# A delta-rule recurrence in units of eight heads by 128 tokens, with its projections kept in DRAM

## The chip, the cores and the metric

One core of one Trainium2 chip. The metric is the device time of one execution in microseconds. The kernel before took 3592.41 us in the median of three runs (3590.86 to 3600.78).

## The reference

Three transformer-like blocks follow each other on one sequence of 1024 tokens by 1024 channels, all in float32. The change lies in the second block. That block normalises its input, projects it (`h @ w_in`, 2816 columns), and splits the result: 1792 columns feed a recurrence of eight heads of 64 channels, 1024 columns feed a gated convolution of 31 taps. Both results, 512 channels each, go through one output projection and are added to the input; then comes a feed-forward part.

```python
def rwkv7_recurrence(r, decay, k, v, a_vec, b_vec):
    def step(S, inp):
        r_t, w_t, k_t, v_t, a_t, b_t = inp
        sa = jnp.einsum('bhvk,bhk->bhv', S, a_t)
        S = S * w_t[:, :, None, :] + sa[..., :, None] * b_t[:, :, None, :] + v_t[..., :, None] * k_t[:, :, None, :]
        y = jnp.einsum('bhvk,bhk->bhv', S, r_t)
        return S, y
...
def second_block(x, ...):
        h = rmsnorm(x, norm_mix_g[l])
        p = h @ w_in[l]
        p_rwkv = p[..., :D_RWKV_IN]
        p_rwkv = p_rwkv + (token_shift(p_rwkv) - p_rwkv) * shift_mu[l]
        p_conv = p[..., D_RWKV_IN:]
        y_rwkv = rwkv7_group(p_rwkv, ...)
        y_conv = conformer_conv_group(p_conv, ...)
        x = x + jnp.concatenate([y_rwkv, y_conv], axis=-1) @ w_out[l]
        h = rmsnorm(x, norm_mlp_g[l])
        x = x + jnp.square(jax.nn.relu(h @ w_ff1[l])) @ w_ff2[l]
```

`rwkv7_group` makes r, k and v (512 columns each), the decay and the gates from the projection, runs the recurrence, normalises each head's output, adds a bonus term and multiplies by a gate.

## The kernel before

Activations lie channel-major: 128 channels on the partitions, tokens along the free dimension, in two halves of 512 tokens. A projection of 128 columns over one half is eight steps over the input channels, three matmuls each (operands are split into a high and a low part, `split`, lines 127 to 129), 24 matmuls of 128x512. `shift_mix` (line 1146 on) runs one such projection in eight parts and mixes it with its neighbour token: ScalarE scales it (L1160), VectorE adds the shifted copy (L1161). The weights come by `w_a`: one load of 512 KB on the SyncE queue (L139, two buffers `raw`), then the split on ScalarE (L128) and GpSimd (L129).

The recurrence is computed in chunks of 64 tokens, and its work in *units*. Before, a unit is one of two groups of four heads (two tiles of 128 channels) by 256 tokens, that is four chunks; a half has four units, group 0 twice, then group 1 twice. There are eight units. Each has

- a *preparation*, `rwkv_pre` (line 1200 on): decay, gates and norms, then the score matrices inside a chunk (`sa`, `sb`, L1285 and L1289), transposes, and `chunk_inverse` (L1437 to L1472), which inverts the eight 64x64 triangles with products of 32x32 blocks; its last matmuls are L1328. It yields some 31 times, and nearly every step needs the one before;
- a *chain*, `rwkv_chain` (line 1333 on): for each of the four chunks, state times `ar` (L1345), add (L1348), times the inverse (L1351), copy to `uv` (L1353, L1354), state update (L1359, L1363, with a product on GpSimd, L1356) and the output into `yp` (L1368, L1369). The state `z` goes from chunk to chunk and from unit to unit of a group;
- an *end*, `rwkv_post`: statistics on ScalarE and GpSimd (L1375 to L1390), transposes (L1401), gate, and a store into the DRAM tensor `mixd`.

In `mixers_2` (line 1559 on) three kinds of work are woven together. `drive` takes one step of each of its streams in turn, by the estimated numbers of steps `STEPS`: the chain and end of unit u, and the preparation of unit u+1. Beside them it feeds parts from a list, `work`, through `feed`; `SLOTS` says how many projections' worth of eight parts each drive gets (nine drives: preparation 0, then the eight chains). It also takes convolution taps from the list `taps`, `TAPS` in a drive: each convolution projection leaves 31 of them, two thirds on VectorE (L1511), one third on ScalarE and GpSimd (L1505, L1506). The steps of the streams have priority over the fed parts when the compiler orders the engines' queues.

The list `work` before: the two low-rank projections `L[0]`, the six projections `P[0]` of group 0, the convolution's `C[0]` to `C[3]` with `P[1]` between them, a reload of the second half's input, `L[1]`; then `P[2]` with the layer norm of the convolution's first half beside it (`("beside", N[0])`: one step of `conv_norm` for every six parts, `SIDE`; at `("join",)` the rest of the norm is run with no part beside it); then `C[4]` to `C[7]` with `P[3]`; then the output projection of the first half, `O[:4]`, with the second norm `N[1]` beside it; then a join, `mixed1` (the convolution's memory is given up, the second half's residual and mixed values are loaded) and `O[4:]`. `conv_norm` first takes the taps that are left, four a step, then transposes, normalises and stores eight blocks of 128 channels by 256 tokens with one buffer `cu` (L1548 to L1554, store L1571).

Eight projections' worth of parts run before the first drive. The output projection of the second half leaves out two of its eight channel tiles, those of the last unit; `ffn_2` adds them after the recurrence (L1775 to L1781). The projections r, k and v of a group stay in SBUF (`rkv`, six buffers of 128x2x512).

## Time and profile before

| what | value |
|---|---|
| median of three runs | 3592.41 us |
| the profiled execution, its own time | 3586.6 us |
| its span, first to last instruction | 3584.8 us |
| mean granted TensorE clock | 0.965 |
| TensorE busy | 96% |
| second block's recurrence with its projections | 1456 to 2237 us of the span |

The page's second part gives busy shares in 40 slices of 89.6 us each; slices 17 to 25 hold the stage of the change. A view by stretches gives, for each stretch of time, its length, each engine's busy time and count, the granted TensorE clock (1.00 is full speed, 0.50 half), the share of time that the DMA engines were busy, and GB/s. A view by groups gives for each line the busy time, the mean duration in ns of one instruction, and the idle time of its engine before it with what ended it. The timeline gives start and length of single instructions.

### The profile page before, as it was taken

The page shows a single profiled execution, that of the slowest core. Times are in us where ns is not written, and L with a number is a line of the kernel's source. Part 1 is how long each engine was busy: PE and PEld are TensorE (multiplying, and loading weights), DVE is VectorE, ACT ScalarE, POOL GpSimd, SP SyncE. Part 2 cuts the span into 40 slices and gives each one's busy share as a digit, 9 for nine tenths or more (in the row PEclk, how much of TensorE's full clock was granted, in tenths as well). Part 3 has the DMA queues.
Part 4 walks back from the last instruction along what each step waited for, and adds up shares of the span by engine and source line. Part 5 has one row for each costly group of instructions (what it writes and reads, how often), then busy time and mean ns, then how long its engine had stood idle before and what let it go on. Part 6 is the DMA issues. An engine that isn't in the chain of part 4 may idle for free.

```text
span 3584.8 us, 53990 instructions
## 1 busy us (share of the span) xinstructions
PE 3431.0 (96%) x22218; PEld 2742.5 (77%) x22218; DVE 2137.7 (60%) x3062; ACT 1152.0 (32%) x2191; POOL 1514.8 (42%) x1270
## 2 busy tenths in 40 slices
PE   8999889989999999999999998999999999998998
PEld 5877778777888887777776777888888887776877
DVE  7556785877577577675455643544444334577583
ACT  2322212232222222544444534312211134444561
POOL 3455552674344444554434634433333334344120
PEclk9999999999999999999979998999999999999999
DMA  5210035011111112412111223222222121110132
GB/s 190 71 52 24 27 124 212 30 42 48 47 47 48 47 47 71 156 43 83 44 40 45 65 74 121 92 75 72 71 68 65 50 77 51 42 33 30 51 106 77
DMA packets 256387, 247.26 MB, mean 69 GB/s; under 512 B 9490, under 2 KB 201598, under 8 KB 256138
## 3 DMA queue, kind: packets, MB, share of 16 engines
q1 hardware_dynamic: 256140, 243.80, 21.1%
q8 instruction: 175, 2.87, 0.3%
q14 instruction: 72, 0.59, 0.1%
HBM read 217.27 MB, written 26.49 MB: 68 GB/s over the span
## 4 chain that ended last, share of the span: by engine, by line
PE 69%; DVE 8%; POOL 3%; issue 3%; ACT 2%; DMA 1%; POOLq 0%; DVEq 0%; SPq 0%; ACTq 0%
PE mps L174 11%; PE mps L176 10%; PE mps L175 10%; PE dps L174 5%; PE dps L176 5%; PE dps L175 5%; PE mps L1148 3%; PE mps L1150 2%; PE mps L1149 2%; DVE cacc L927 2%; POOL hl L129 1%; PE ps L1285 1%; PE ps L1444 1%; PE yp L1988 1%; PE mps L1621 1%
## 5 line engine op out<-in xcount | busy, mean ns | idle before, releaser
L129 POOL TENSOR_TENSOR hl<-raw,hl 128x1024 fp32r<-128x1024 f32 x247 | 619.2, 2509 | 828.5 <-ACT hl L128 625.6
L174 PE MATMUL mps<-xt,hl 128*128 128x512 f32 x1888 | 755.0, 401 | 13.0 <-DVE cacc L940 8.1
L175 PE MATMUL mps<-xt,hl 128*128 128x512 f32 x1888 | 745.0, 395 | 0.0
L176 PE MATMUL mps<-xt,hl 128*128 128x512 f32 x1888 | 744.9, 395 | 0.0
L128 ACT CAST hl<-raw 128x1024 fp32r<-128x1024 f32 (+1 forms) x260 | 270.5, 1042 | 629.6 <-PE dps L176 443.9
L174 PEld LDWEIGHTS mps<-xt,hl 128*128 128x128 f32 x1888 | 358.7, 190 | 94.5 <-DVE cacc L940 8.6
L176 PEld LDWEIGHTS mps<-xt,hl 128*128 128x128 f32 x1888 | 357.7, 189 | 79.2 <-issue 0.9
L175 PEld LDWEIGHTS mps<-xt,hl 128*128 128x128 f32 x1888 | 358.8, 190 | 74.8 <-issue 1.0
L927 DVE SCALAR_TENSOR_TENSOR cacc<-apad,cols,cacc 128x1024 f32<-128x1024 f32 x176 | 345.5, 1967 | 112.3 <-ACT cacc L921 108.6
L174 PE MATMUL dps<-hl,hid 128*128 128x512 f32 x832 | 326.5, 393 | 1.5 <-DVE x L956 1.3
L176 PE MATMUL dps<-hl,hid 128*128 128x512 f32 x832 | 326.0, 392 | 0.6 <-POOL hid L849 0.6
L175 PE MATMUL dps<-hl,hid 128*128 128x512 f32 x832 | 326.2, 392 | 0.0
L1810 DVE TENSOR_TENSOR x<-x,dps 128x512 f32<-128x512 f32 x224 | 152.9, 687 | 175.2 <-PE dps L176 175.2
L174 PEld LDWEIGHTS dps<-hl,hid 128*128 128x128 f32 x832 | 156.1, 188 | 37.1 <-DVE x L956 1.7
L176 PEld LDWEIGHTS dps<-hl,hid 128*128 128x128 f32 x832 | 156.2, 188 | 35.7 <-POOL hid L849 1.1
L175 PEld LDWEIGHTS dps<-hl,hid 128*128 128x128 f32 x832 | 156.2, 188 | 34.3
L1797 DVE TENSOR_TENSOR ftmp<-ftmp 128x512 f32<-128x512 f32 x64 | 60.5, 947 | 177.2 <-ACT ftmp L1796 177.2
L1148 PE MATMUL mps<-xt,hl 128*128 128x512 f32 x352 | 162.3, 461 | 0.0
L174 PE MATMUL mps<-hl,xt 128*128 128x512 f32 (+1 forms) x368 | 140.1, 384 | 5.4 <-ACT xt L240 1.7
L1150 PE MATMUL mps<-xt,hl 128*128 128x512 f32 x352 | 144.5, 411 | 0.0
L1149 PE MATMUL mps<-xt,hl 128*128 128x512 f32 x352 | 144.3, 410 | 0.0
L175 PE MATMUL mps<-hl,xt 128*128 128x512 f32 (+1 forms) x368 | 139.3, 380 | 1.3 <-DVE hl L129 1.3
(518 smaller groups left out, 6480.0 us busy)
## 6 DMA issues: line engine op xcount, KB each, us to landing
raw<-in_w_in_dram SPq DMA_DIRECT2D x108, 512.0 KB
raw<-in_w_ff_dram SPq DMA_DIRECT2D x64, 512.0 KB
raw<-in_ffn_up_dram SPq DMA_DIRECT2D x44, 512.0 KB
adar<-in_ada_w_dram SPq DMA_DIRECT2D x32, 512.0 KB
raw<-in_w_out_dram SPq DMA_DIRECT2D x30, 512.0 KB
adar<-in_w_ada_dram SPq DMA_DIRECT2D x48, 256.0 KB
raw<-in_ffn_down_dram SPq DMA_DIRECT2D x22, 512.0 KB
xd<-x SPq DMA_DIRECT2D x16, 512.0 KB
```

Of the source, the lines that this page charges most:

```text
L128: nc.scalar.copy(hl[:, 0], raw)
L129: (low or nc.gpsimd).tensor_tensor(out=hl[:, 1], in0=raw, in1=f32(hl[:, 0]), op=ALU.subtract)
L174: self.nc.tensor.matmul(ps, lhsT=sh, rhs=mh, start=(i == 0), stop=False)
L175: self.nc.tensor.matmul(ps, lhsT=sh, rhs=ml, start=False, stop=False)
L176: self.nc.tensor.matmul(ps, lhsT=sl, rhs=mh, start=False, stop=(i == n - 1))
L927: nc.vector.scalar_tensor_tensor(out=acc, in0=pad[:, i // 3:i // 3 + 16, i % 3:i % 3 + 64], scalar=cw[:, i * 22 + j:i * 22 + j + 1], in1=a ...
L1148: nc.tensor.matmul(ps, lhsT=sh, rhs=xt[k][:, 0], start=(k == 0), stop=False)
L1149: nc.tensor.matmul(ps, lhsT=sh, rhs=xt[k][:, 1], start=False, stop=False)
L1150: nc.tensor.matmul(ps, lhsT=sl, rhs=xt[k][:, 0], start=False, stop=(k == 7))
L1285: nc.tensor.matmul(ps[:, c], lhsT=bk4[hp, b, c, h:h + 2].rearrange("p x s -> p (x s)"), rhs=ar4[hp, b, c].rearrange("p x s -> p (x s)"), s ...
L1797: nc.vector.tensor_tensor(out=v, in0=v, in1=v, op=ALU.mult)
L1810: nc.vector.tensor_tensor(out=xs[t][:, c], in0=xs[t][:, c], in1=ps, op=ALU.add)
```

## The change

A unit becomes all eight heads (four tiles of 128 channels) by 128 tokens, that is two chunks. The chain has two chunks a unit with eight heads side by side, one state tile instead of two, and its state update is an addition and a product on VectorE, with nothing on GpSimd. The r, k and v projections are stored in a DRAM tensor `rkvd` as they are made, all twelve of a half before the half's first unit, and a unit loads its 128 tokens of them back. The list of work, `SLOTS`, `TAPS` and `STEPS` change with it, and the second half's output projection now leaves out the last 128 tokens' recurrence channels instead of two channel tiles.

```diff
-SLOTS = (5, 5, 5, 6, 6, 6, 6, 5.5, 6.5)
+SLOTS = (5, 5, 5, 4, 4, 4, 3.5, 3, 8.5)
-STEPS = (20, 30)
-TAPS = 31
+STEPS = (12, 30)
+TAPS = 24
...
+        self.rkvd = dr.tile([1536, 1024], F32, name="rkvd")
...
-            res[0] = pool.tile([128, 512], F32, tag="tw", name="tw", bufs=1)
+            res[0] = pool.tile([128, 512], F32, tag="tw", name="tw", bufs=2)
...
+    def rwkv_proj(self, i, hf, xts, pool, psum, done):
+        out = []
+        def new():
+            out.append(pool.tile([128, 512], F32, tag="rkv", name="rkv", bufs=3))
+            return out[0]
+        yield from self.shift_mix(i, hf, xts, psum, new)
+        self.nc.sync.dma_start(out=self.rkvd[i * 128:(i + 1) * 128, hf * 512:hf * 512 + 512], in_=out[0])
+        done.append(i)
+
+    def rwkv_load(self, u, pool):
+        res = []
+        for n, i in (("k", 4), ("r", 0), ("v", 8)):
+            t = pool.tile([128, 4, 128], F32, tag="in" + n, name="in" + n, bufs=2)
+            self.nc.sync.dma_start(out=t, in_=self.rkvd[i * 128:(i + 4) * 128, u * 128:u * 128 + 128].rearrange("(b p) t -> p b t", p=128))
+            res.append(t)
+        return res
...
-        for b in range(2):
+        for b in range(4):
             nc.scalar.activation(out=sq[:, b], in_=k[:, b], func=ACT.Square, scale=col("k_k", b))
...
-        for b in range(2):
-            nc.vector.tensor_tensor_scan(out=sg[:, b], data0=m2["reset"].rearrange("p c t -> p (c t)"), data1=sg[:, b], initial=0.0,
-                                         op0=ALU.mult, op1=ALU.add)
+        nc.vector.tensor_tensor_scan(out=flat(sg), data0=m2["reset"].rearrange("p c t -> p (c t)"), data1=flat(sg), initial=0.0,
+                                     op0=ALU.mult, op1=ALU.add)
...
+        pairs = [(b, h, hp) for b in range(4) for h, hp in enumerate(hps)]
+        yp = psum.tile([128, 2, 4, 64], F32, tag="y", name="yp")
+        for c in range(2):
+            pc = psum.tile([128, 2, 4, 64], F32, tag="ch", name="pc")
+            for b, h, hp in pairs:
+                nc.tensor.matmul(pc[hp, 0, b], lhsT=ar[hp, 2 * b + c, 0], rhs=z[hp, b], start=True, stop=True)
             yield
+            rh = pool.tile([128, 4, 64], F32, tag="rh", name="rh", bufs=2)
+            nc.vector.tensor_tensor(out=rh, in0=pc[:, 0], in1=of(w1, c), op=ALU.add)
...
-            zg = pool.tile([128, 2, 64], F32, tag="zg", name="zg", bufs=1)
-            nc.gpsimd.tensor_tensor(out=zg, in0=z, in1=glv[:, :, c:c + 1].to_broadcast([128, 2, 64]), op=ALU.mult)
...
+            zn = pool.tile([128, 4, 64], F32, tag="z", name="z", bufs=3)
+            nc.vector.tensor_tensor(out=zn, in0=pc[:, 0], in1=z, op=ALU.add)
+            nc.vector.tensor_tensor(out=zn, in0=zn, in1=of(gl[:, :, None], c).to_broadcast([128, 4, 64]), op=ALU.mult)
...
-        P = [self.rwkv_proj(j % 2, j // 2, xts, lo, psum, projs[j]) for j in range(4)]
+        P = [[self.rwkv_proj(i, hf, xts, lo, psum, done) for b in range(4) for i in (4 + b, b, 8 + b)] for hf in range(2)]
-        work = L[0] + P[0]
+        work = L[0] + P[0][:4]
...
         def pre(u):
+            states[u] = yield from self.rwkv_pre(u % 4, loaded.pop(u), loras[u // 4][0], lw, r, psum)
+            if u < 7:
+                loaded[u + 1] = self.rwkv_load(u + 1, r)
...
-        work += C[0] + P[1][:3] + C[1] + P[1][3:] + C[2] + C[3] + [reload()] + L[1]
-        work += [("beside", N[0])] + P[2] + [("join",)] + C[4] + P[3][:3] + C[5] + P[3][3:] + C[6] + C[7] + [mixed()]
-        work += [("beside", N[1])] + O[:4] + [("join",), mixed1()] + O[4:]
-        more(4 * NPART)
+        work += C[0] + P[0][4:8] + C[1] + P[0][8:] + C[2] + C[3] + [reload()] + L[1]
+        work += [("beside", N[0])] + P[1] + [("join",)] + C[4] + C[5] + C[6] + C[7]
+        work += [mixed(), ("beside", N[1])] + O[:4] + [("join",), mixed1()] + O[4:]
+        for i in range(14 * NPART):
+            more(1)
+            if i % 2 and taps:
+                taps.pop(0)()
+        loaded[0] = self.rwkv_load(0, r)
...
-            for k in (4, 5, 6, 7, 0, 1):
+            for k in (4, 5, 6, 7):
                 self.load_mixed(mts1[k], k, 512, 512)
+            for k in range(4):
+                self.load_mixed(mts1[k], k, 512, 384)
...
-                terms = self.terms_b(xt, t, [hls[0][0]], 4, 256) + self.terms_b(xt, t, [hls[1][0]], hls[1][1], 256, 4)
+                terms = self.terms_b(xt, t, hls[:1], 4, 256, 4)
+                if hf == 0 or t < 3:
+                    terms += self.terms_b(xt, t, hls[1:], 4, 256)
...
-            hls = [self.w_b(a["w_out_2"][0], 256, 2, ch * 512, 512) for ch in range(2)]
...
+            for c0 in range(0, 1024, 256):
+                c = slice(c0, c0 + 256)
+                ps = psum.tile([128, 512], F32, tag="mm", name="mps")[:, :256]
+                self.mm3(ps, self.terms_b(mts, 3, [self.w_b(a["w_out_2"][0], 0, 4, c0, 256)], 4, 256))
+                nc.vector.tensor_tensor(out=xs[7][:, c], in0=xs[7][:, c], in1=ps, op=ALU.add)
```

In the preparation the loops over two tiles of 256 tokens become loops over four tiles of 128 (ScalarE's squares, tanh and scalings, VectorE's products by `k_k` and `r_k`, the low-rank matmuls), and the scan over the decay becomes one instruction instead of two. `chunk_inverse` only indexes its input in another way. The order of the work is now: eighteen projections' worth of parts before the first drive (`L[0]`, all of the first half's twelve, `C[0]`, `C[1]`), with one tap after every second part; then `C[2]`, `C[3]`, the reload, `L[1]`, all twelve of the second half beside the first layer norm, `C[4]` to `C[7]`, and the output projection as before.

## The prediction

> **What bounds the kernel now.** I read the page's totals first, then busy time by stretches, then single lines inside them.

> ```profile
> span 3584.8 us, 53990 instructions
> ...
> PE 3431.0 (96%) x22218; PEld 2742.5 (77%) x22218; DVE 2137.7 (60%) x3062; ACT 1152.0 (32%) x2191; POOL 1514.8 (42%) x1270
> ...
> PEclk9999999999999999999979998999999999999999
> ```

> TensorE (PE) is the bound by count, at full clock except in slices 20 to 24. Those slices hold the stage that the change rewrites, from 1456 to 2237 us. The next view cuts it: the projections ahead of the recurrence (first row), a piece of it with nothing else in it, the preparation of unit 0, the seven stretches in which chain u runs beside preparation u+1, the last chain, one hole, and a piece of the output projection. A stretch ends where the last matmul group of a preparation, line 1328, starts. Columns: length, busy us (count) of PE, PEld, DVE, ACT, POOL, then granted clock and DMA.

> ```profile
> 1456.00:1504.00 48.00, 48.00 (x232) 40.20 (x231) 19.73 (x32) 24.98 (x37) 27.57 (x27) 1.00 0.67 225
> 1480.00:1494.00 14.00, 14.00 (x63) 11.61 (x62) 4.08 (x9) 6.31 (x10) 5.71 (x7) 1.00 0.77 271
> 1504.00:1556.00 52.00, 46.43 (x742) 33.94 (x742) 39.79 (x68) 24.51 (x41) 31.39 (x24) 0.97 0.19 55
> 1556.00:1635.00 79.00, 78.07 (x1008) 55.97 (x1006) 42.57 (x86) 35.07 (x89) 37.08 (x32) 0.94 0.13 39
> 1635.00:1710.00 75.00, 73.94 (x1022) 53.07 (x1017) 48.87 (x94) 39.38 (x96) 43.88 (x39) 0.98 0.30 93
> 1710.00:1799.00 89.00, 86.61 (x1019) 62.59 (x1019) 40.05 (x87) 33.73 (x87) 33.95 (x32) 0.90 0.15 43
> 1799.00:1901.00 102.00, 100.83 (x1040) 75.19 (x1034) 53.05 (x110) 40.80 (x99) 39.86 (x36) 0.75 0.15 45
> 1901.00:1990.00 89.00, 85.90 (x1028) 61.28 (x1028) 45.36 (x88) 36.98 (x92) 39.18 (x32) 0.90 0.14 40
> 1990.00:2075.00 85.00, 78.88 (x1093) 61.10 (x1095) 63.10 (x110) 46.68 (x107) 58.63 (x45) 0.94 0.23 76
> 2075.00:2157.00 82.00, 77.94 (x1170) 65.47 (x1166) 37.28 (x84) 26.01 (x76) 22.18 (x23) 0.96 0.20 66
> 2157.00:2237.00 80.00, 67.38 (x551) 59.57 (x548) 27.62 (x56) 30.16 (x81) 31.80 (x35) 0.81 0.39 132
> 1821.00:1853.00 32.00, 30.93 (x313) 23.00 (x308) 18.61 (x47) 7.25 (x16) 4.83 (x7) 0.56 0.10 30
> 2207.00:2212.00 5.00, 5.00 (x44) 5.00 (x43) 2.24 (x3) 2.62 (x4) 2.76 (x4) 1.00 0.78 289
> ```

> PE looks busy nearly throughout, but what fills it differs. Undisturbed, a 128x512 matmul costs 14.00/63 = 0.222 us, so a part (three matmuls, an eighth of a projection) costs 0.67 us and a projection 5.33. A 128x256 one costs 5.00/44 = 0.114 us. Inside the units the same parts cost more, and the clock is down to a mean of 0.91 over the seven rows. The same stretches for line 1150 alone (busy PE, PEld; its count is the number of parts fed) show how unit length goes with parts:

> ```profile
> 1556.00:1635.00 79.00, 16.72 (x41) 7.99 (x41) 0.94 0.13 39
> 1635.00:1710.00 75.00, 16.30 (x40) 7.81 (x40) 0.98 0.30 93
> 1710.00:1799.00 89.00, 19.68 (x47) 9.54 (x47) 0.90 0.15 43
> 1901.00:1990.00 89.00, 20.78 (x49) 9.88 (x48) 0.90 0.14 40
> ```

> Units of 40 and 41 parts take 77 us on average, units of 47 and 49 take 89: 12 us for 7.5 parts, 1.6 us a part.

> **The change, part by part.**

> *1. Fewer parts beside each unit, more ahead.* The slots for the seven stretches go from 5, 5, 6, 6, 6, 6, 5.5 to 5, 5, 4, 4, 4, 3.5, 3, eight parts each: 40, 40, 32, 32, 32, 28, 24. Ten more projections (18 instead of 8) run before unit 0. What is one part worth inside a unit? From below 0.67, from above the 1.6 of the fit (which also holds other differences between those units).

> ```profile
> L1148 PE MATMUL mps<-xt,hl x352: 389/398/796, 1456.3 to 2035.0; 128*128 128x512 f32 x176
> ```

> ```profile
> L1148 PE MATMUL mps<-xt,hl 128*128 128x512 f32 x284 | 135.5, 477 | 0.0
> L1150 PE MATMUL mps<-xt,hl 128*128 128x512 f32 x284 | 118.0, 416 | 0.0
> L1149 PE MATMUL mps<-xt,hl 128*128 128x512 f32 x284 | 117.8, 415 | 0.0
> ```

> The first row is min/median/max over all parts, the others are the means inside the recurrence. The first matmul of a part takes 0.08 us over the median, the other two 0.02 each: 0.12 us for coming in between small matmuls. With 0.67/0.91 = 0.74 for the clock I take 0.86, nearer to the lower end because it is built from these rows. The rest of a unit is then 77 - 40.5 x 0.86 = 42.2 us. The number of recurrence matmuls hardly changes (chain 80 a unit before, 80 after; the inverse the same; six more a unit where 256-wide ones become two of 128), so this rest is kept. The third row of the seven has 89 - 42.2 - 47 x 0.86 = 6 us over for the convolution's layer norm beside it; I give that to the second new unit. New stretches: 76.6, 82.6, three of 69.7, 66.3, 62.8: 497 us for 601 before. The hole of 32 us (1821 to 1853, clock 0.56, not one part in it) is gone in this sum: 12 projections instead of 6 lie beside the first layer norm, 84 steps of the feeder, so 14 steps of the norm, and it needs about twelve.

> *2. The ten projections ahead.* At least 5.33 us each, at most 48.00/8 = 6.0, which holds 40 other matmuls. I take 5.7: **+57**. New there are a store of 256 KB behind each and convolution taps on DVE, ACT and POOL. Does the store, waiting on SP for its DVE result, hold up the weight load queued behind it?

> ```profile
> 1498.17 0.75 DVE L1161 SCALAR_TENSOR_TENSOR rkv<-mps,cols,rkv 128x511 f32<-128x511 f32 x1 [4.63 <-ACT rkv L1160]
> 1498.83 0.15 DVE L1167 COPY last<-mps 128x1 f32<-128x1 f32 x1
> 1499.15 2.39 POOL L129 TENSOR_TENSOR hl<-raw,hl 128x1024 fp32r<-128x1024 f32 x1 [3.04 <-ACT hl L128]
> 1501.57 0.37 SPq L139 DMA_DIRECT2D raw<-in_w_in_dram  x1
> ```

> The result is there at 1498.92, the next load's buffer only at 1501.54: the store goes first and the load loses nothing. If taps push DVE back by over 2.6 us, or POOL's split by as much, the cover is gone and each us lands on PE; the 6.0 is for that. The three buffers of the projections live 17 us, a store a few.

> *3. Loads of a unit.* Three loads of 256 KB, issued after the preparation before. The nearest row is another load of that size:

> ```profile
> 2176.54 0.32 SPq L856 DMA_DIRECT2D xt<-mixd  x1
> ...
> 2179.66 0.62 ACT L857 CAST xt<-xt 128x512 fp32r<-128x512 f32 x1 [1.56 <-DMA xt<-mixd]
> ```

> 3.1 us from issue to use. Unit 0 sees some of it (**+2**; 0 to 9 if all three come in turn); later ones are loaded a unit ahead. Only unit 4 needs what was stored last; its cover is the parts of the fourth convolution projections.

> *4. The chain.* Two steps a unit instead of four, each twice as wide; GpSimd's product (32 times) goes, ScalarE has two more calls at five places.

> ```profile
> PE yp L1369 <- DVE uv L1353: 6.5, 5, 2.2
> PE pc L1351 <- DVE rh L1348: 1.5, 2, 1.1
> ```

> These are the waits of PE for the chain from 1512 to 2240 (total, times, longest). Half as many steps: **-4**; between 0 and -8. The extra ScalarE calls cost the bound nothing while ACT is busy 35 of 79 us; uncovered I estimate 1 us a unit.

> *5. The last stretch.* Slots go from 6.5 to 8.5. The second layer norm comes due with fewer taps taken: 24 instead of 31 a drive. Counting feeds, its taps end with the seventh stretch, where they ended some 20 feeds before it; so both its halves, not one, fall behind the last preparation, with only the chain beside them.

> ```profile
> 2169.62 0.32 SPq L1571 DMA_DIRECT2D mixd<-cu  x1
> ...
> 2174.71 0.32 SPq L1571 DMA_DIRECT2D mixd<-cu  x1
> ...
> 2179.69 0.32 SPq L1571 DMA_DIRECT2D mixd<-cu  x1
> ...
> 2183.90 0.32 SPq L1571 DMA_DIRECT2D mixd<-cu  x1
> ...
> 2197.08 0.48 PE L1401 MATMUL ps<-ident,y 64*64 64x64 f32 x4 [7.11 <-ACT y L1390]
> ...
> 2200.32 0.58 PE L1621 MATMUL mps<-hl,xt 128*128 128x256 f32 x1
> ```

> A block of the norm takes (2183.90-2169.62)/3 = 4.8 us, eight 38; then 16 us until the output projection starts (2200.32, after reloads); then 112 triples at 0.34 = 38 and a few us of remains: 96 against 80, **+16**. What goes is PE's 7.11 us wait for the last unit's statistics, which now lie beside the norm. Bounds: -2 if the norm ends as early as today, +35 if taps are left over as well.

> *6. After the stage.* 48 matmuls of 256 instead of 512: -48 x 0.108 = -5. Two more weight splits (2.4 us of POOL each) for +2: **-3**; at worst +3.

> **Sum:** 497 - 601 + 57 + 2 - 4 + 16 - 3 = -36. The profiled execution took 3586.6 us (span 3584.8), so 3551; the median of the runs shown, 3592.4, lies 5.8 higher: **3556**.

> **The rivals.**

> *Steeper units.* A part costs the full 1.6 us: units of 32 parts take 63, of 28 57, of 24 51, together 458 instead of 497: 3517. For it: the fit itself. Against: the dense price is 0.67, and one of its two long units has the layer norm in it.

> *Units that don't shrink (slower).* The preparation is one chain of some thirty dependent steps, PE to DVE, ACT or POOL and back. If that sets the length, fewer parts only bare its waits: seven units at 77, one with 6 more, are 545, and the sum is +12: 3604; with a unit of 78 it is 3611. It decides from a mean unit of (601 - 68)/7 = 76 us. For it: none of the rows is under 75, and preparation 0 alone, with 40 parts, took 52. Against: that same 52, far under 76.

> *The clock.* In the hole, PE was busy 30.93 of 32 us and yet the granted clock was 0.56. There were only small matmuls. So stretches without parts run slow, and the change thins the parts inside a unit from 48 to 32. With a clock of 0.83, midway between the mean 0.91 and the 0.75 of the row with the hole, 493 us become 540: +11, 3603. Against: the hole itself goes.

> [...]

> **How the numbers follow.** Forecast 0.57, steeper 0.18, not shrinking 0.11, clock 0.14. A measurement of this kernel tells about 0.3% (11 us) from no change: 3582 to 3603. Faster: 0.52 of the forecast's and the 0.18; same: 0.05 and 0.10 of the clock's; slower: 0.11 and 0.04. The range takes in all but the steeper case's lower half (0.08) and the tops of the slow ones (0.07): 3512 to 3606; the forecast's own is 3535 to 3582.

> **What would show it.** Eighteen projections end near 1560 us at clock 1.00, with no PE wait for hl; otherwise step 2 is wrong. Units of 32 parts are near 70 us: at 63 or 77 a rival holds. No 30 us without parts before the last stretch. In the last stretch eight norm blocks follow each other, and the clock there is low. Wrong altogether it would be if the compiler's order of the two streams costs more than parts do.

## The result, and the profile after

The changed kernel takes 3676.6 us (median of four runs, 3673.1 to 3679.2) against 3591.8 for the kernel before on the same chip: a ratio of 1.023, 95% interval 1.0211 to 1.0248. It is 85 us slower; 36 us faster was forecast, and the range ended at 3606. The views below are each of one profiled execution; the spans of these two, 3677.4 and 3584.8, are 92.6 us apart, 8 more than the medians. From the page of the changed kernel (span, busy time, granted clock in slices):

```profile
span 3677.4 us, 54391 instructions
...
PE 3504.2 (95%) x22362; PEld 2814.7 (77%) x22362; DVE 2145.3 (58%) x3018; ACT 1168.1 (32%) x2259; POOL 1505.0 (41%) x1233
...
PEclk9999999999999999988877776999999999999999
```

TensorE (PE) is busy for 73 us more than before with 144 more records, and the dip of the clock is longer and deeper. The same cut of the stage as in the prediction, for the changed kernel: the projections ahead, the preparation of unit 0, seven stretches of chain and preparation side by side, the last chain. A stretch ends where line 1333 (before: 1328) first starts. Columns: length, busy us (count) of PE, PEld, DVE, ACT, POOL, then granted clock and DMA.

```profile
1456.00:1556.00 100.00, 100.00 (x464) 83.38 (x462) 57.06 (x87) 52.29 (x74) 73.67 (x55) 1.00 0.58 188
1556.00:1616.80 60.80, 53.14 (x774) 39.63 (x772) 43.18 (x78) 32.17 (x60) 40.17 (x32) 0.92 0.53 168
1616.80:1707.00 90.20, 87.31 (x1017) 64.14 (x1015) 39.39 (x78) 35.00 (x95) 31.43 (x24) 0.83 0.17 51
1707.00:1792.50 85.50, 81.78 (x1023) 60.98 (x1021) 36.62 (x78) 31.80 (x91) 22.48 (x19) 0.86 0.18 57
1792.50:1879.10 86.60, 85.72 (x1009) 63.10 (x1007) 36.13 (x75) 31.03 (x90) 21.32 (x18) 0.80 0.21 65
1879.10:1965.00 85.90, 82.78 (x988) 61.17 (x987) 52.98 (x86) 38.08 (x101) 38.02 (x30) 0.78 0.13 38
1965.00:2061.20 96.20, 90.19 (x997) 68.01 (x995) 69.73 (x109) 49.44 (x118) 56.50 (x44) 0.70 0.18 56
2061.20:2143.20 82.00, 78.78 (x1082) 65.02 (x1080) 33.37 (x66) 26.40 (x81) 19.16 (x15) 0.79 0.14 45
2143.20:2231.50 88.30, 86.10 (x1040) 71.01 (x1036) 26.34 (x60) 23.05 (x75) 14.88 (x13) 0.75 0.14 45
2231.50:2329.70 98.20, 73.90 (x632) 65.81 (x631) 32.35 (x63) 36.03 (x88) 36.44 (x40) 0.77 0.34 119
```

The seven stretches take 614.7 us where 497 was forecast (before: 601), and PE idles about 6 us at most in any of them. What differs most from before is their clock. The whole of the seven in one row, before and after:

```profile
1555.80:2156.70 600.90, 582.07 (x7336) 434.59 (x7334) 330.04 (x657) 258.50 (x643) 274.76 (x238) 0.90 0.18 57
```

```profile
1616.80:2231.50 614.70, 592.67 (x7140) 453.43 (x7138) 294.56 (x549) 234.80 (x649) 203.79 (x161) 0.79 0.16 51
```

A mean clock of 0.79 is 263 us at half clock, for 116 before. The sum of the prediction, term by term:

```
term                                     forecast   measured
seven stretches                         601 -> 497  600.9 -> 614.7   (+14 for -104)
ten projections ahead, loads (2, 3)        +59      +61.0  (line 1328/1333 of unit 0: 1555.8 -> 1616.8)
last stretch (5)                           +16      +18.8  (79.4 -> 98.2)
after the stage (6)                         -3       -1.0
```

(The chain's -4, term 4, would lie inside the seven stretches.) One term is wrong, by 118 us. The next view groups PE's instructions inside the seven stretches of the changed kernel: line, shape, count, busy us, mean ns, idle time before them.

```profile
L1433 PE MATMUL ps<-ix,sa 32*32 32x32 f32 x1792 | 79.4, 207 | 1.2 <-DVE ix L1443 1.0
...
L1399 PE MATMUL ps<-ident,y 64*64 64x64 f32 x224 | 48.5, 313 | 0.0
```

Before, the same two groups (lines 1437 and 1401) had as many records and took far less. The transposes then met the inverse's other group of products (line 1444; now L1440, busy for 26.5 us), so all three belong to the comparison: 111 us together before, 154 now.

```profile
L1444 PE MATMUL ps<-iq,iy 32*32 32x32 f32 x1792 | 44.9, 201 | 0.2
...
L1437 PE MATMUL ps<-ix,sa 32*32 32x32 f32 x1792 | 33.4, 197 | 0.0
L1401 PE MATMUL ps<-ident,y 64*64 64x64 f32 x224 | 32.3, 276 | 3.0 <-ACT y L1390 2.9
```

The order of time in the changed kernel shows why (start, duration, line, shape, records):

```profile
1950.00 0.31 PE L1433 MATMUL ps<-ix,sa 32*32 32x32 f32 x2
1950.23 0.47 PE L1399 MATMUL ps<-ident,y 64*64 64x64 f32 x2
1950.64 0.31 PE L1433 MATMUL ps<-ix,sa 32*32 32x32 f32 x2
1950.88 0.47 PE L1399 MATMUL ps<-ident,y 64*64 64x64 f32 x2
1951.28 0.31 PE L1433 MATMUL ps<-ix,sa 32*32 32x32 f32 x2
```

Each of these small f32 matmuls leaves two records (the 4,040 of the first experiment left 8,080), so this is one transpose of the chain's end and one small matmul of the other stream's inverse in turn, 0.64 us a pair. In the code both streams' steps are issued at the same rank, `high_priority(offset=0)`, and where groups of both are ready the compiled order takes one of each. Records of one shape follow each other in 0.05 us (64x64 at full clock, 0.10 at half) or 0.01 (32x32, at both); a step from 64x64 to 32x32 takes 0.148 us at full clock and 0.241 at half, back 0.121 and 0.166 (medians over the seven stretches). Such steps between the chain with its end and the inverse (its two large groups, lines 1433 and 1440, before 1437 and 1444) are 455 in the changed kernel, 80 us, and 290 before, 47 us (the expectations below name 434 and 234, those of the four commonest pairs of lines). A group of the chain now has 8 matmuls, its output 16, where it had 4 and 8; and the sixteen transposes at its end now meet a group of the inverse in every unit: 220 changes between lines 1399 and 1433, 31 a unit, for 134 before (1401 and 1444), 19 a unit. Stretches of over 3.4 us without a wide matmul (256 columns or more) are 26 with 231 us together, for 14 with 102 us.

```
weighted columns in a window    windows   next window at half clock
under 1,500                        114       114
1,500 to 3,250                     189        78
over 3,250                       1,796         0
```

Both limits were chosen on these two traces. On the traces of the eleven experiments below other than the bursts the same limits hold: 506 of 507 windows under 1,500 were followed by half clock, 517 of 1,120 between them, and 4 of 9,874 over 3,250.

So the theory for the experiments is: PE need not idle to lose the clock (of the 192 half-clock windows 95 followed one with under 0.1 us of waiting); few columns in a window are enough, and a run of small matmuls that change shape at each step has few. That gives two causes to tell apart: **order** (the alternation that twice as wide steps lengthen) and **thinness** (fewer wide parts beside the units). The rivals: dependent steps set a unit's length, or a part simply costs its price.

### The profile page after: what moved, and what is told of

Its sections match the earlier page's. It is cut to its first block, busy times and chain, and to the rows that moved or that the text cites. A ratio compares the mean times of both kernels' runs of the same rounds, so it can differ in the third digit from the quotient of the medians.

```text
span 3677.4 us, 54391 instructions
## 1 busy us (share of the span) xinstructions
PE 3504.2 (95%) x22362; PEld 2814.7 (77%) x22362; DVE 2145.3 (58%) x3018; ACT 1168.1 (32%) x2259; POOL 1505.0 (41%) x1233
## 4 chain that ended last, share of the span: by engine, by line
PE 70%; DVE 8%; POOL 2%; ACT 2%; issue 2%; DMA 2%; SPq 0%; POOLq 0%; DVEq 0%; ACTq 0%
PE mps L175 10%; PE mps L177 10%; PE mps L176 10%; PE dps L175 5%; PE dps L177 5%; PE dps L176 5%; PE mps L1149 3%; PE mps L1150 2%; PE mps L1151 2%; DVE cacc L928 2%; PE ps L1433 2%; PE ps L1292 1%; PE ps L1399 1%; PE mps L1618 1%; PE yp L1989 1%
## 5 line engine op out<-in xcount | busy, mean ns | idle before, releaser
L130 POOL TENSOR_TENSOR hl<-raw,hl 128x1024 fp32r<-128x1024 f32 x249 | 627.1, 2520 | 920.5 <-ACT hl L129 716.3
L129 ACT CAST hl<-raw 128x1024 fp32r<-128x1024 f32 x262 | 274.4, 1048 | 625.8 <-PE dps L177 442.1
L1149 PE MATMUL mps<-xt,hl 128*128 128x512 f32 x352 | 163.6, 465 | 0.0
L1150 PE MATMUL mps<-xt,hl 128*128 128x512 f32 x352 | 148.1, 421 | 0.0
```

The lines of the kernel that those rows point to most:

```text
L129: nc.scalar.copy(hl[:, 0], raw)
L130: (low or nc.gpsimd).tensor_tensor(out=hl[:, 1], in0=raw, in1=f32(hl[:, 0]), op=ALU.subtract)
L1149: nc.tensor.matmul(ps, lhsT=sh, rhs=xt[k][:, 0], start=(k == 0), stop=False)
L1150: nc.tensor.matmul(ps, lhsT=sh, rhs=xt[k][:, 1], start=False, stop=False)
```

## The experiments

In the first four the weighting by rows was not yet in the theory: their texts speak of plain columns with a limit of about 2,400. "Changes of shape" below are those between chain and inverse in the seven stretches; "half" is the time at half clock there, "waits" PE's idle time.

### Bursts of small matmuls alone

```
+ for i in range(2400): one(q4[i % 4], i // 4, 32)      # burst 0
+ for i in range(800):  one(q4[0], i, 32)               # burst 1
+ for i in range(600):  one(q2[i % 2], i // 2, 64)      # burst 2
+ for i in range(120):  one(q2[i % 2], i // 2, 64); one(q4[i % 4], i // 4, 32)   # burst 3
```

> The changed kernel with four bursts of independent small TensorE matmuls put between the projections ahead of unit 0 (they only read the identity and write a scratch PSUM tile; nothing on another engine stands behind them). Burst 0: 2,400 of 32x32 over the four row groups in turn; burst 1: 800 of 32x32 in one row group; burst 2: 600 of 64x64; burst 3: 120 pairs of 64x64 and 32x32 in turn. Theory 'columns' (TensorE's granted clock in one window of 3.41 us follows the number of moving columns that it took in the window before; below about 2,400 it is halved): burst 0 at 11 ns each is 9,900 columns a window, full clock; burst 2 at 51 ns is 4,300, full clock; burst 3 at 148 + 121 ns a pair is 1,200, half clock after its first window and then 241 + 166 ns a pair, although TensorE waits for nothing; burst 1 at 30 to 50 ns is 2,200 to 3,600, near the limit. Theory 'waits' (the clock is halved where TensorE is not busy): all four at full clock. Theory 'small matmuls alone' (any stretch without wide matmuls is at half clock): all four at half clock. Time: 3677 + 26 + 30 + 31 + 32 (or 49 at half clock in burst 3), some 3795 to 3815.

The four bursts, one row each (length, busy, counts, clock as above):

```profile
1500.00:1635.00 135.00, 69.97 (x4784) 65.16 (x4773) 0.00 (x0) 0.00 (x0) 1.13 (x1) 0.52 0.05 13
1660.00:1739.00 79.00, 79.00 (x1486) 79.00 (x1484) 3.71 (x5) 2.17 (x3) 5.84 (x6) 0.50 0.03 9
1761.00:1796.00 35.00, 34.93 (x1189) 34.79 (x1190) 0.00 (x0) 0.00 (x0) 0.64 (x1) 1.00 0.07 19
1819.00:1890.00 71.00, 71.00 (x446) 50.80 (x444) 0.69 (x1) 0.96 (x2) 4.10 (x5) 0.50 0.06 16
```

Bursts 1 and 3 keep PE busy for 79.00 of 79.00 and 71.00 of 71.00 us and run at 0.50: being busy did not hold the clock. Burst 2, small matmuls too, runs at 1.00: smallness alone didn't lose it. The alternation of burst 3 did, with no other engine involved: 120 pairs took 75 us, 0.62 each. Burst 0 was to be at full clock and was not: 121 records a window are 3,900 plain columns, but 970 weighted by their 32 of 128 rows. It also waited for 65 us on nothing that the profile shows, so it decides least. Weighted, bursts 1, 2 and 3 have about 510, 3,700 and 430 columns a window, on the right sides of the table. The time, 4017 us in a single run, was 200 above what was expected: bursts 0, 1 and 3 at half clock, and the 65 us.

### The kernel before, with thinner parts

```
- nc.tensor.matmul(ps, lhsT=sl, rhs=xt[k][:, 0], start=False, stop=(k == 7))
+ if not self.thin:      # thin: beside units 0 to 6
+     nc.tensor.matmul(ps, lhsT=sl, rhs=xt[k][:, 0], start=False, stop=(k == 7))
```

> The kernel before the change, its order and its feeding kept, but each part fed beside units 0 to 6 has two matmuls instead of three (the product of the weight's low half with the activation's high half is left out there; the output loses precision). Some 250 matmuls of 512 columns and 120 of 256 go: 250 x 0.222 + 120 x 0.114 = 69 us at the undisturbed price, 92 at the mean price of a part in those units (0.87 us for three). Theory 'price' (a part costs its own time wherever it is): 3592 - 69 to 3592 - 92, 3500 to 3523, half-clock time in the seven stretches as before, 116 us. Theory 'columns' (thin stretches lose the clock): half-clock time rises to over 180 us and the kernel wins less than 40 us: 3552 or more. Theory 'dependent steps' (a unit has a length of its own): 3585 to 3592, with new TensorE waits of 60 us or more and no more half clock than those waits explain.

3556.7 us (three runs), ratio 0.9891, 0.9847 to 0.9935. The seven stretches:

```profile
1559.60:2147.90 588.30, 554.29 (x6977) 399.02 (x6975) 333.06 (x659) 255.69 (x643) 272.63 (x239) 0.78 0.19 58
```

Some 69 us of wide matmuls (at the undisturbed price) went, and the stretches got 12.6 us shorter: half rose from 116 to 255 us, waits only from 19 to 34, and the changes of shape fell to 139. (The row is from the slowest of the three runs, 9 us above their median.) The time lies in the band of theory "columns". Thinness without more alternation, in the kernel before, takes the clock from 0.90 to 0.78. Theory "price" is out. It is also the sharpest sign against the forecast's own value of a part.

### The changed kernel, with thicker parts

```
- yield from self.parts(ps, hl, xts[hf])
+ if twice:              # ten projections; likewise half of the first O blocks
+     yield from self.parts(ps, hl, xts[hf])
+     yield
+ yield from self.parts(ps, hl, xts[hf])
- SLOTS = (5, 5, 5, 4, 4, 4, 3.5, 3, 8.5)
+ SLOTS = (5, 7, 7, 6, 6, 5.5, 5.25, 4.5, 8.75)
- SIDE = 6
+ SIDE = 9
```

`SIDE` goes up with the parts, so that the convolution's norm advances beside them about as before.

> The changed kernel with about half as many parts again beside units 0 to 6: ten of the projections of the second half, and every second token block of the first half's output projection, are done twice into the same PSUM tile (the second overwrites the first, the output is the same), with the slots raised to match (7, 7, 6, 6, 5.5, 5.25, 4.5). Extra work: 240 matmuls of 512 and 192 of 256, 240 x 0.222 + 192 x 0.114 = 75 us at the undisturbed price. Theory 'columns': the half-clock time in the seven stretches (263 us) falls below 150, what the clock gives back pays for most of the extra work, the stretches stay between 84 and 92 us, total 3665 to 3705. Theory 'price': a part costs 0.67 to 1.0 us: 112 more parts are +75 to +112, total 3752 to 3789, half-clock time not much changed. Theory 'dependent steps': total 3677, and TensorE's waits (22 us in the seven stretches) go to zero.

3739.8 us, 63 above the changed kernel, in none of the bands. Half fell only from 263 to 230 us; the changes of shape stayed at 438. "Dependent steps" is out (58 us longer in the seven stretches). My reading was that more parts don't bring the clock back (0.83, for 0.79) as long as they can't get between the alternating matmuls; it was tried below.

### Holding the last transposes

```
+ turn(*todo[0])         # waits for the last of ScalarE's eight results
+ with self.tc.issue_after(self.anchor()):
+     for x in todo[1:]: turn(*x)
```

> The changed kernel with the sixteen 64x64 transposes at the end of a chain held until the last of ScalarE's eight results is there, and then issued one behind the other, instead of two at a time between the 32x32 matmuls of the other stream. In the trace of the changed kernel a step from a 64x64 to a 32x32 matmul takes 148 ns (241 at half clock) and back 121 (166), against 51 between two of 64x64. The 224 transposes of the seven stretches take 40.7 us there. Theory 'order of the streams' (these changes of shape cost time that grouping gives back): 224 x 0.05 = 11 us instead, -25 to -30, and with the clock that the denser windows get back up to -45: 3632 to 3652. Theory 'nothing' (the held transposes put off the end of the chain as much as they save): 3670 to 3685. Rival 'slower': the chain's end gates the next chain's start and the unit gets longer: over 3690.

3671.3 us, ratio to before 1.022 (1.0192 to 1.0247), the changed kernel's being 1.023: "nothing". But the edit did not do what it meant: changes of shape are 455, as without it, and the transposes still alternate with the inverse, matmul by matmul. So it is not ScalarE's pace that makes them alternate; they do it when all are ready.

### TensorE's order fixed

```
- with tc.high_priority(offset=0):
+ with tc.high_priority(offset=0), tc.issue_after(self.anchor()):
      next(streams[i][0])
```

> The changed kernel with TensorE's order fixed as it is written: each step of either stream is queued behind the last TensorE instruction before it, so that two groups of matmuls of the two streams no longer go two by two. In the changed kernel's trace of the seven stretches, steps from the one stream's groups to the other's (lines 1399, 1394, 1368, 1369 against 1433) are 434 changes of array shape, 76 us; in the kernel before 234, 39 us. Stretches of small matmuls longer than 3.4 us without a wide one between them sum to 231 us there (before: 102). Theory 'two by two' (twice as many heads in a step make the runs in which the streams alternate twice as long, longer than one window of the clock): the 434 fall below 60, the stretches over 3.4 us below 130 us, half-clock time from 263 to 150 or less, total 3580 to 3625. Theory 'thin' (the parts are too few, whatever the order): the changes of shape go but the half-clock time stays over 220 us; total 3630 to 3655. Rival 'bared waits': in a fixed order TensorE stands where the other order went round a wait: its waits in the seven stretches rise from 22 us to over 80, total 3677 or more.

3645.3 us, ratio 1.0143 (1.0127 to 1.0158), in the band of theory "thin":

```profile
1620.30:2176.20 555.90, 495.52 (x7119) 380.74 (x7117) 284.98 (x549) 234.43 (x650) 204.94 (x161) 0.84 0.18 56
```

Changes of shape: 2. The seven stretches fall by 59 us to 556, half to 181, while waits rise from 22 to 60 us; the last stretch grows by 18 (116.5 for 98.2). Half clock lies between the two theories (150 or less, over 220), so each has a share: in the seven stretches the alternation cost more than the waits that its removal bares.

> The kernel before the change with TensorE's order fixed as it is written, the same edit as for the changed kernel. There the alternation is 234 changes of shape, 39 us, and half-clock time in the seven stretches is 116 us, 51 of them in the one with the hole. Theory 'two by two': -25 to -45, 3547 to 3567, less than the changed kernel wins by the same edit, since it has half as much to win. Rival 'bared waits': 3592 or more.

The same edit in the kernel before costs 61 us: 3654.9, ratio 1.0164 (1.0136 to 1.0191). The rival came: waits 19 to 70 us, half up to 198, the seven stretches 663. In this kernel, with less alternation to remove, the fixed order loses.

### The chain ranked ahead

```
- with tc.high_priority(offset=0):
+ with tc.high_priority(offset=100 if i == 0 else 0):
      next(streams[i][0])
```

> The changed kernel with the chain's stream ranked ahead of the preparation's (by 100 places) instead of level with it; nothing else is fixed. If level rank is what makes the groups go two by two, the 434 changes of shape between the streams fall below 100, half-clock time falls below 200 us and the total lies between 3600 and 3650. If the alternation comes from results that arrive two at a time (ScalarE's eight calls), only the last transposes still alternate (lines 1399 against 1433 keep over 150 of their 220), total 3645 to 3670. If the preparation now comes late and becomes the unit's length: over 3677.

3590.4 us (ten runs), ratio 0.9986 (0.997 to 1.0003): 86 us less than the changed kernel by one number in one line, and below the expected 3600 to 3650. In the seven stretches (from the slowest of the ten runs, 9 us above their median):

```profile
1620.50:2152.90 532.40, 501.21 (x7146) 389.46 (x7144) 286.00 (x551) 233.72 (x650) 203.40 (x161) 0.84 0.19 59
```

```profile
L1433 PE MATMUL ps<-ix,sa 32*32 32x32 f32 x1792 | 25.9, 196 | 1.1 <-DVE ix L1443 1.1
...
L1399 PE MATMUL ps<-ident,y 64*64 64x64 f32 x224 | 8.0, 221 | 0.0
```

The same records of lines 1433 and 1399 are busy for 34 us in place of 128. In the order of time the sixteen transposes now follow each other in 1.1 us:

```profile
1911.27 1.15 PE L1399 MATMUL ps<-ident,y 64*64 64x64 f32 x32
1912.35 0.74 PE L1433 MATMUL ps<-ix,sa 32*32 32x32 f32 x62
```

Changes of shape: 12, half 174. The rank also lets the chain run earlier; that this is not the whole of it is shown by the fixed order, which leaves the rank alone and still gets 59 of the 82 us. PE's busy time there falls almost alike under both edits, from 592.7 to 495.5 and 501.2 us. An estimate from these rows splits the 91 us of the ranked kernel: 443 changes of shape fewer, each 0.13 us at full clock for 0.03 within one shape (the mean of the two shapes), are some 46 us, and 89 us less at half clock are another 44. So the steps themselves cost about as much as the clock that they lose.

> The kernel before the change with the chain's stream ranked ahead of the preparation's by 100 places. Theory 'two by two': -15 to -40, 3552 to 3577. If the preparation comes late: 3592 or more.

3559.2 us, ratio 0.9906 (0.9886 to 0.9926), as expected: changes of shape from 290 to 74, the seven stretches from 601 to 574. So ranking wins 27 us there in the kernel before and 82 in the changed one. (Half clock is 126 us here, for 116. The estimate above explains only 18 of the 38 us by which PE's busy time falls, so ranking does more than remove these steps.) With both ranked, the change still loses 31 us (3590.4 against 3559.2).

### Thicker parts once the alternation is gone

> The changed kernel with the chain ranked ahead (3590) and the doubled parts of the earlier experiment: 75 us more of wide matmuls at the undisturbed price beside units 0 to 6. Without the ranking the doubling cost 63 us and half-clock time in the seven stretches went only from 263 to 230 us; the reading is that parts can't come in where the two streams alternate. Theory 'columns', with the alternation gone: half-clock time falls from 174 to below 110 us, total 3625 to 3645. Theory 'price': 3665 to 3702 with half-clock time over 150.

The edit is the doubling (with `SIDE` at 9) and the rank together. 3636.8 us: 46 us for the 75 us of wide work, where it had been 63. The seven stretches without the doubling stand above; with it:

```profile
1612.10:2190.20 578.10, 557.59 (x7494) 433.21 (x7493) 291.06 (x551) 236.66 (x650) 203.87 (x163) 0.90 0.18 54
```

Half falls from 174 to 117 us (110 was the line that I drew) and the clock is back at 0.90. Now the parts get in, and give back more than a third of their price. Its fourth stretch takes 72.7 us at clock 0.98 with 144 wide matmul records; without the doubling it took 78.6 at 0.78 with 96.

### Four projections moved back beside the units

```
- work = L[0] + P[0][:4]
+ work = L[0] + P[0]
- for i in range(14 * NPART):
+ for i in range(10 * NPART):
```

> The changed kernel with the chain ranked ahead (3590), and with four of the eighteen projections (the first two blocks of the convolution) moved from ahead of unit 0 back beside units 0 to 2, so that these have 52, 52 and 44 parts in place of 40, 40 and 32; convolution taps 50 a stretch. Ahead of unit 0 that takes off 4 x 5.6 = 22 us. Theory 'price' (0.86 to 1.0 us a part): 32 x 0.86 to 1.0 = +28 to +32 beside the units, total 3595 to 3600. Theory 'columns' (a part in a thin stretch pays for itself through the clock): half-clock time in the stretches of units 0 to 2 (51 us) falls below 30 and they take at most 15 us more, total 3575 to 3585.

3607.1 us, above both bands. Ahead of the seven stretches 29 us went, the stretches grew by 67, the last one shrank by 32, and 11 came after the stage. The convolution's norms (SIDE 6 to 5) and its taps (24 to 50) had to move with it, so the 67 are not the price of 32 parts; this run settles nothing about it.

### Towards a better kernel

```
  for b in range(4):
      for h, hp in enumerate(hps):   # A, A
          nc.tensor.matmul(yp[hp, c, b], lhsT=ar[hp, 2 * b + c, 1], rhs=z[hp, b], start=True, stop=False)
+     seq.enter_context(self.tc.issue_after(self.anchor()))
      for h, hp in enumerate(hps):   # B, B
          nc.tensor.matmul(yp[hp, c, b], lhsT=sb[:, h, 2 * b + c], rhs=uv[:, 2 * b + c, h], start=False, stop=True)
- SIDE = 6               # the last two lines in the second kernel only
+ SIDE = 4
```

> The changed kernel with the chain ranked ahead (3590), and in the chain's output the two products of a pair of heads in the order A A B B (both 64x64 products, then both 128x64 ones) instead of A B A B. With the chain ranked ahead, changes of shape between lines 1368 and 1369 are 179 in the seven stretches, 33.6 us, 0.188 us each, against 0.05 between two of one shape. Halved they give 90 x 0.138 = 12 us, with what the clock gives back up to 25: 3565 to 3580. Rival 'nothing': those runs stand in half-clock windows anyway and the group's fixed order costs a wait, 3584 to 3596.

3562.6 us, ratio 0.9914 (0.9892 to 0.9937), a little more than expected: changes of shape inside the chain from 195 to 89, half from 174 to 140, the seven stretches 506.6 us. With two edits of order and nothing else the changed kernel stands near the forecast's numbers (3556, and 497 for the seven stretches). That is a coincidence: the forecast was of a kernel without these edits, and the kernel before gains by such edits too, as the next run shows.

> The kernel before with the chain ranked ahead (3559), the chain's products in the order A A B B, and the convolution's layer norm advanced at every fourth feed instead of every sixth, so that the first norm's twelve steps fit beside its 48 feeds. 141 changes of shape between lines 1368 and 1369, 24.9 us, halved: 70 x 0.13 = 9 us; the stretch with what is left of the hole, 89 us against 82 to 86 beside it: 5 us. 3540 to 3552. Rival: the norm now takes VectorE and PSUM from the preparation while the wide matmuls run, 3559 or more.

3525.5 us (five runs), ratio 0.9811 (0.9789 to 0.9833), better than expected and the fastest of all. The seven stretches and the last one, first without the two new edits, then with them:

```profile
1555.20:2129.60 574.40, 544.55 (x7316) 413.63 (x7314) 333.49 (x658) 256.49 (x643) 273.56 (x238) 0.89 0.19 60
2129.60:2207.80 78.20, 65.20 (x568) 57.28 (x566) 24.36 (x55) 29.50 (x80) 32.30 (x34) 0.80 0.39 132
```

```profile
1562.10:2120.20 558.10, 518.49 (x7346) 393.32 (x7344) 349.90 (x672) 260.02 (x649) 279.30 (x244) 0.91 0.21 65
2120.20:2172.30 52.10, 51.27 (x535) 45.98 (x534) 13.98 (x35) 21.46 (x65) 22.03 (x19) 1.00 0.34 117
```

The larger gain, 26 us, is in the last stretch, and not in the hole where I looked for it: the second norm now ends before the last preparation, and PE no longer stands between its blocks. 13 us come back after the stage; why was not looked into, and the two edits were not run apart.

## Why the prediction was wrong, step by step

*The failing step* is in part 1: "The number of recurrence matmuls hardly changes (...), so this rest is kept". The number is kept, the order isn't. The rest of a unit (small matmuls, from start to start) was 44.5 us on average before and is 51.4 after, and the 231 parts that are left in the seven stretches cost 1.01 us each where the 310 cost 0.87 (a part of 256 columns is counted as half). What the runs showed in its place:

- Order, some 55 of the 118 us: the two streams' groups alternate matmul by matmul, and the runs of it are longer than a window of the clock (between lines 1399 and 1433 they last 3.7 to 10.7 us each, a window 3.41). Ranking wins 82 us in the seven stretches; 27 of them the kernel before had to win too, so its lengths, from which the forecast took its rest, already held that much. That the runs grew by the wider groups and by where the chain's end falls is read from the two traces; it wasn't tried by itself. The prediction ended on the words that it would be wrong altogether "if the compiler's order of the two streams costs more than parts do". The trace of before had it already: the 134 steps between lines 1401 and 1444. I gave that case no chance of its own.
- What is left, some 62 us: with both kernels ranked, the change takes 42 us off the seven stretches instead of 104. The rest of a unit is then indeed kept (38.6 us before, 39.3 after). But 80 parts fewer take only 48 us with them (274 to 226 us of wide matmuls), 0.60 each where the forecast counted 0.86. The thin run of before (69 us of wide matmuls out, 12.6 us off the stretches) and the dense run of the ranked kernel (75 in, 46 us on) point the same way: half clock went from 116 to 255 us where the wide work was taken out, and from 174 to 117 where it was put in, so the clock paid part of the price. This accounts for some 20 of the 62 us; another 13 are the hole, whose stretch ranking alone shortens in the kernel before, from 102 to 89 us. How the remainder splits is open.

*The rivals.* "The clock" named the right resource and the right sign, at a chance of 0.14, but sized it from a mean (0.83) over unchanged work, and blamed the thinner parts alone; the clock was 0.79, and the time 74 us above its 3603. "Units that don't shrink" came nearest in its lengths (77 and 78 for 82 to 96), but for a reason that the runs exclude, so that is luck: dependent steps don't set the length, since the ranked run has units of 67 to 85 us with the same steps, and PE waits for only 22 of the 614.7 us. "Steeper units" is excluded.

*What held.* The last matmul of the eighteen projections starts at 1558.1, at clock 1.00 (100.00 of 100.00 us busy to 1556). The +61.0 for +59 are two small misses that partly cancel: the projections end 55 us later (57 forecast), and unit 0's preparation takes 6 us more (2 forecast, at most 9). The last stretch: +18.8 for +16, at clock 0.77. Before it no stretch without a part is longer than 17.3 us; the hole is gone, as the sum had it. The chain's waits (lines 1355, 1361 and 1369) are some 6 us in the seven stretches: too small to judge its -4.

*Waits and the clock.* Long waits came with half clock: of the 59 windows of the two traces in which PE waited 1.7 us or more, 58 were followed by it. But a wait was not needed: bursts 1 and 3 are wholly busy at 0.50, and ahead of 95 of the 192 half-clock windows PE waited for under 0.1 us. Why a step from 64x64 to 32x32 takes 0.148 us, for 0.05 between two of 64x64, no run shows.

*What stays open.* Between 1,500 and 3,250 weighted columns the table doesn't decide (78 of 189 windows), so it is not shown that the chip goes by this measure. The 31 us that the change still loses with ranked streams were not split into norm, projections ahead and thinness by runs of their own. The experiments on order compare whole kernels, so what ranking does besides ending the alternation is not separated.

## What to carry to other kernels

Where two streams of small matmuls share TensorE, look at their order in time before pricing either: give them different ranks, so that a group of one shape runs through, rather than fix the whole order, which bared waits here (22 to 60 us and 19 to 70; it won 31 us in one kernel and lost 61 in the other). Where the clock fell without the wide matmuls, they cost less than their own time (0.90 to 0.78 with 69 us of them out, and 12.6 us won in the seven stretches), so don't use a slope of length against parts in such a stretch backwards. And when a step is made wider, ask how long PE then goes without the wide work that used to come between two steps.

## What the runs showed that was not expected

- The clock did not follow the profile's busy time: 114 of 114 windows under 1,500 weighted columns were followed by half clock, none of 1,796 over 3,250 was, and two shapes of matmul in turn were enough to get under 1,500 on an engine that did not wait (burst 3: some 430 columns a window, busy for 71.00 of 71.00 us, clock 0.50).
- A burst of 2,400 independent 32x32 matmuls over the four row groups was busy for 69.97 of 135.00 us. The rest are waits for nothing that the profile names; the rows of the bursts of one row group and of 64x64 have next to none (79.00 of 79.00 and 34.93 of 35.00 us busy).
